# ConvFFN on one Trainium2 core: the last pair's block sums made by VectorE instead of by adding stores

## The chip, the cores and the metric

The kernel runs on one core of a Trainium2 chip. The metric is the device time of one execution in microseconds (us); less is better. TensorE (PE in the profile, its weight loads PEld) does the matmuls, VectorE (DVE) and ScalarE (ACT) the elementwise work, GpSimd (POOL) and SyncE (SP) mostly issue DMA transfers.

## The reference, cut to what matters

The program is a decoder trunk of two layers (attention mixes, then a ConvFFN in each). Only the ConvFFN is touched here, and it runs once in each layer:

```python
def conv_ffn(h, w_up, conv_w, conv_b, w_down):
    T = h.shape[1]
    a, b = jnp.split(h @ w_up, 2, axis=-1)
    a_pad = jnp.pad(a, ((0, 0), (CONV_WIDTH - 1, 0), (0, 0)))
    a = sum(a_pad[:, j:j + T] * conv_w[j] for j in range(CONV_WIDTH)) + conv_b
    return (jax.nn.silu(a) * b) @ w_down
```

Here T = 1024 tokens, the model width is 1024 and the inner width FFN_DIM is 2816, so 22 tiles of 128 channels.

## The kernel before

Both matrix products of the ConvFFN are done by a Strassen-like scheme with seven products in place of eight. The names `T1` to `T4` and `B11` to `B22` are the right-hand blocks and block sums of such a scheme; each product has its number (1 to 7).

**The up product.** A `Up` object ("unit") makes one tile of 128 inner channels of `a` and of `b` for both halves of the tokens (512 each). Its seven products are the methods `p1` to `p7`; each is 12 matmuls of 128x512 (four blocks of the contraction, and three matmuls a block, because every operand is split into a high and a low part). `sums` makes the sums of the weights that products 6, 7, 3 and 5 need, four DVE additions of 128x512 (L1042 to L1045). `split67` and `split35` split those sums into high and low parts. `p5` ends with a DVE instruction `summed` (L1103) that drains its PSUM tile `fw` into `s1`; product 3 adds on top of the same PSUM tile, so it may not start before that drain. `run` puts these calls of a unit and of the next one (`nxt`) in order.

**The gated blocks.** A unit ends with two gated blocks of 128x512, `c[0]` and `c[1]`, one for each half of the tokens (`gate`, DVE, L1160 and L1161). Units go in pairs, 11 pairs of a layer: the first of a pair has `mate` None, the second has the first as `mate`. Each pair leaves seven blocks in DRAM (`gb_d`): B11, T1, B21, B22, T2, T3, T4. Four of these are sums of up to four gated blocks. The kernel before makes the sums in DRAM: `store` writes a block (SP queue, L1167), and `more` adds another onto it (POOL queue, L1171, a DMA with `accum_op=ALU.add`). T4 gets all four blocks of its pair.

**The down product** is a loop over 77 steps, 7 products times 11 pairs, in the order of `DOWN` (L419): T4, B11, T2, B21, T3, T1, B22. A step is 12 matmuls (L1402 to L1404) into PSUM tiles `dn`. `load(i)` issues from SP, six steps ahead (`AHEAD`), the block `bl` from `gb_d` (L1266) and, in the first product, half of a weight tile `wb`, in the second a weight tile `wa` of 128x1024. `operand(i)`, three steps ahead (`READY`), makes the operands `da` (weights) and `db` (block): the high parts on ACT (L1326, L1331), the low parts on DVE (L1327, L1332). In the second product DVE also adds `wa` onto `wb` (L1294). Step 10 is the last step of the first product: it reads T4 of the last pair. Step 11 is the first that needs a `wa`. Four loads of `x` (L1352) go out between the load of step 10 and that of step 11.

**What sets the order.** The code names dependences and a scheduler places the instructions of each engine in one fixed list; an engine works its list strictly in order, so an instruction that waits holds up all behind it. SP's list too is one queue.

Of the kernel before, what the change touches and what calls it, by code (L numbers as in the profile page):

```python
# [11 lines left out]
ALU = mybir.AluOpType  # L12
# [22 lines left out]
def kernel(  # L35
# [25 lines left out]
    nc = tc.nc  # L61
# [19 lines left out]
    def PS(s="ps"):  # L81
        return pp.tile([P, HT], F32, tag="ps", name=nm(s))
# [7 lines left out]
    def hs(half):  # L90
        return slice(half * HT, (half + 1) * HT)
# [46 lines left out]
    def follow(n, after, reason):  # L138
        tc.add_manual_dep(
            n.ins,  # L140
            after.ins.name,
            mybir.DependencyInfo(mybir.DependencyClass.NoSync, mybir.DependencyReason.DATA),
            reason=reason,
        )
# [5 lines left out]
    def back_to_exp(after):  # L150
        follow(nc.scalar.preload_act_table_set(LN_EXP), after, "table")
# [827 lines left out]
    def ffn(l, blocks_, after):  # L979
# [25 lines left out]
        class Up:  # L1005
# [5 lines left out]
            def load(self, k=None):  # L1011
                if k is None:
                    self.load(0)
                    k = 1
                if k == 0:
                    self.raw = slot("raw", 2, raws)
                t = self.raw[k]
                for j in (1, 0) if self.early else (0, 1):
                    nc.sync.dma_start(t[:, hs(j)], w_up[l, j * NF + self.i, :, hs(k)])
# [85 lines left out]
            def p4(self):  # L1105
                ps = PS("fv")
                self.product(ps, 4, True, True)
                nc.vector.tensor_tensor(self.t, ps, self.t, ALU.add)
                self.ended = self.gate(0, self.t)
                if self.mate is None:  # L1110
                    self.stored = self.store(self.c[0], "B11", "T1", "T2", "T4")
                else:
                    self.stored = self.store(self.c[0], "B21")
                    self.more(self.c[0], "T4")

            def p3(self):
                self.product(self.W, 3, False, True)
# [28 lines left out]
            def end(self):  # L1146
                self.c.append(self.taps(self.q, self.edge))
                self.act(1)
                self.gate(1, self.s1)
                if self.mate is None:  # L1150
                    self.more(self.c[1], "T1", "T2", "T4")
                    self.store(self.c[1], "T3")
                else:
                    self.store(self.c[1], "B22")
                    self.more(self.c[1], "T2", "T3", "T4")

            def gate(self, half, t):
                c = self.c[half]
# [16 lines left out]
        def each(group, *whats):  # L1175
            for what in whats:
                for u in group:
                    getattr(u, what)()

        def ahead(then, after):  # L1180
            if after is not None:
                after.load(1)
            if then is not None and then.early:
                then.again()

        def run(u, last, then, after):
            nxt = [then] if then is not None else []
            if u.s1 is None:
                u.p1()
            u.p6()  # L1190
            if after is not None:
                after.load(0)
            if u.early:
                each(nxt, "direct")
                then.p1()
                each(last, "end")
                u.split35((then.kept, u.opened))
                ahead(then, after)
                u.p7()
                u.taps0()  # L1200
            else:
                u.p2()
                each(last[:1], "end")
                u.split35((u.kept, u.opened))
                ahead(then, after)
                u.p7()
                each(nxt, "direct")
            u.act0()
            each(nxt, "sums")
            u.p5()  # L1210
            for v in nxt:
                v.split67((u.acted, u.drained))
            if not u.early:
                each(last[1:], "end")
            u.p4()
            u.p3()
# [6 lines left out]
        seq = pair + order[:-1]  # L1223
        for n, u in enumerate(seq):
            u.n, u.mate = n // 2, seq[n - 1] if n % 2 else None
        each(pair, "load", "direct")
        each(pair, "p1")
        pair[0].p2()
# [18 lines left out]
        last = pair  # L1247
        for u, then, after_ in zip(order, order[1:], order[2:] + [None]):
            run(u, last, then, after_)
            last = [u]  # L1250
# [10 lines left out]
        tt = nc.vector.tensor_tensor  # L1261
# [146 lines left out]
        def down():  # L1408
            ps = {}
            for i in range(AHEAD):  # L1410
                load(i)
            for i in range(READY):
                operand(i)
            each(last, "end")
            back_to_exp(silu[0])
            yield 0.0
            for i, (p, n) in enumerate(steps):
                r = DOWN[p][0]
                if r == 3 and n == NP - TAIL:
                    break  # L1420
                if i + AHEAD < len(steps):
                    load(i + AHEAD)
                if n == 4 and p < 4:
                    fetch_x(*((0, range(4, 8)), (1, range(4)), (0, range(4)), (1, range(4, 8)))[p])
                which = "AB"[p % 2] if p < 5 else "B"
                if n == 0 and r not in (2, 3):
                    ps[which] = [PS("dn") for _ in range(4)]
                bank = ps[which]
                for m in range(4):
                    product(i, bank, (m,))  # L1430
                    if n == NP - 1:
                        if r == 5:
                            evac(r, m, bank[m])
                        else:
                            pend.append((r, m, bank[m]))
                if i + READY < len(steps):
                    operand(i + READY)
                if n != NP - 1 and pend:
                    evac(*pend.pop(0))
                yield 2.7  # L1440
            end_ = len(steps) - 1
            segs_ = [(t0 - HT, w) for t0, w in ends if t0 >= HT]
            bank = ps["B"]
            for t0, w in segs_:
                c = slice(t0, t0 + w)
                for m in range(4):
                    for i in range(end_ + 1 - TAIL, end_ + 1):
                        product(i, bank, (m,), c, i == end_)
                    xv = xs[m][:, HT + t0 : HT + t0 + w]
                    tt(xv, bank[m][:, c], xv, ALU.add)  # L1450
                    norm = nn[[e[0] for e in ends].index(HT + t0)]
                    if l == 0:
                        nc.scalar.dma_start(x_d[m, :, hs(1)], xv)
                    if l == 1 and m == 3:
                        norm.add_last(xv)
                    else:
                        norm.add(xv)
                    yield 0.65 * TAIL * w / HT
# [549 lines left out]
```

## Time and profile before

| what | us |
|---|---|
| median of 3 runs | 2266.38 (2264.17 to 2266.48) |
| profiled execution | 2264.45 |
| its span, first to last instruction | 2262.6 |
| PE busy | 2212.7 |
| DVE busy | 1713.2 |
| ACT busy | 1115.7 |
| POOL busy | 341.0 |

Times in the rows are microseconds from the start of the span. The first layer's down product begins at 844.80, the second's at 2029.89. In a row of the timeline the first number is the start, the second the duration; what stands in brackets is the engine's idle time before it and what ended it. A busy time of PE counts a matmul until its modelled end; matmuls overlap, and their starts, about 0.2265 us apart at full clock, are the better measure.

### The profile page before, as it was taken

To read this page: it belongs to the slowest core of one execution; us is meant where nothing else is said; L and a number is where in the kernel's file an instruction comes from. 1 tells how busy PE (TensorE), PEld (TensorE's weight loads), DVE (VectorE), ACT (ScalarE), POOL (GpSimd) and SP (SyncE) were. 2 spreads that over 40 slices of the span, in tenths; PEclk is the share of its full clock that TensorE was granted. 3 is DMA by queue.
4 is the path that set the end of the run, shared out by engine and by line. 5 is a ranking of instruction groups with operands and counts; after the bars stand their busy time and mean duration, and the time that the engine had idled before them with its cause. 6 is when DMAs were issued, how large, how long until landed. Compare 5 with 4: busy or idle time off the path is not lost.

```text
span 2262.6 us, 32372 instructions
## 1 busy us (share of the span) xinstructions
PE 2212.7 (98%) x11522; PEld 1844.6 (82%) x11522; DVE 1713.2 (76%) x3093; ACT 1115.7 (49%) x2085; POOL 341.0 (15%) x419
## 2 busy tenths in 40 slices
PE   9999999999999998999999999999999999999998
PEld 7888887777888887888888888888777888887886
DVE  6886876888777767877756778866988777767877
ACT  5564464543333334455544688874543333334445
POOL 1321300011111110000203223420012111110000
PEclk9999999999999999999999999999999999999999
DMA  6332246457866659543421111036457866659533
GB/s 226 103 103 87 64 164 206 139 168 191 195 159 154 147 137 325 182 135 131 145 83 49 50 46 38 8 115 209 141 168 192 195 161 145 162 137 325 163 97 112
DMA packets 161120, 325.60 MB, mean 144 GB/s; under 512 B 18173, under 2 KB 24910, under 8 KB 160958
## 3 DMA queue, kind: packets, MB, share of 16 engines
q1 hardware_dynamic: 130430, 263.11, 35.4%
q0 software_dynamic: 25776, 52.03, 13.4%
q10 hardware_dynamic: 4752, 8.39, 1.0%
q8 instruction: 90, 1.47, 0.3%
q14 instruction: 72, 0.59, 0.1%
HBM read 211.27 MB, written 112.20 MB: 143 GB/s over the span
## 4 chain that ended last, share of the span: by engine, by line
PE 76%; DVE 12%; DMA 5%; ACT 4%; issue 3%; SPq 0%; POOL 0%; DVEq 0%; ACTq 0%; POOLq 0%
PE dn L1403 5%; PE dn L1402 5%; PE dn L1404 5%; PE fx L1058 3%; PE fx L1060 3%; PE fx L1059 3%; PE fw L1058 3%; PE fw L1060 3%; PE fw L1059 3%; PE op L195 2%; PE op L196 2%; PE op L194 2%; DMA wu<-in_w_up_dram 2%; PE fy L1060 2%; PE fy L1059 2%
## 5 line engine op out<-in xcount | busy, mean ns | idle before, releaser
L1171 POOL DMA_DIRECT2D gb_d<-fc x154 | 134.0, 1130 | 913.1 <-DVE fc L1161 267.3
L1402 PE MATMUL dn<-db,da 128*128 128x512 f32 (+1 forms) x628 | 244.4, 389 | 10.2 <-ACT db L1331 10.2
L1403 PE MATMUL dn<-db,da 128*128 128x512 f32 (+1 forms) x628 | 243.6, 388 | 1.8 <-DVE db L1332 1.8
L1404 PE MATMUL dn<-db,da 128*128 128x512 f32 (+1 forms) x628 | 243.0, 387 | 0.0
L1022 ACT ACTIVATE Ah<-wu 128x1024 fp32r<-128x1024 f32 x124 | 130.2, 1052 | 120.1 <-PE fv L1059 55.0
L1023 DVE TENSOR_TENSOR Al<-wu,Ah 128x1024 fp32r<-128x1024 f32 x124 | 151.1, 1220 | 7.2 <-ACT Ah L1022 6.1
L1402 PEld LDWEIGHTS dn<-db,da 128*128 128x128 f32 x628 | 118.9, 189 | 36.0 <-ACT db L1331 11.9
L1058 PE MATMUL fw<-B,Ah 128*128 128x512 f32 x352 | 138.0, 392 | 4.7 <-DVE s L1103 4.7
L1403 PEld LDWEIGHTS dn<-db,da 128*128 128x128 f32 x628 | 118.8, 189 | 27.6 <-DVE db L1332 3.6
L1060 PE MATMUL fw<-B,Al 128*128 128x512 f32 x352 | 138.0, 392 | 0.0
L1404 PEld LDWEIGHTS dn<-db,da 128*128 128x128 f32 x628 | 118.7, 189 | 23.6
L1059 PE MATMUL fw<-B,Ah 128*128 128x512 f32 x352 | 137.1, 390 | 0.0
L1332 DVE TENSOR_TENSOR db<-bl,db 128x512 fp32r<-128x512 f32 x154 | 106.1, 689 | 36.7 <-ACT db L1331 36.1
L1331 ACT ACTIVATE db<-bl 128x512 fp32r<-128x512 f32 x154 | 95.4, 619 | 28.5 <-PE dn L1404 15.5
L194 PE MATMUL op<-om,wor 128*128 128x512 f32 x256 | 101.7, 398 | 0.8 <-ACT om L230 0.8
L195 PE MATMUL op<-om,wor 128*128 128x512 f32 x256 | 100.0, 391 | 0.9 <-DVE om L231 0.9
L196 PE MATMUL op<-om,wol 128*128 128x512 f32 x256 | 99.7, 390 | 0.0
L1144 ACT ACTIVATE fc<-fc 128x512 f32<-128x512 f32 x88 | 54.3, 626 | 74.1 <-DVE fc L1125 60.6
L1125 DVE SCALAR_TENSOR_TENSOR fc<-q,cs,fc 128x511 f32<-128x511 f32 x88 | 65.8, 748 | 24.4 <-ACT fc L1123 24.4
L1058 PEld LDWEIGHTS fw<-B,Ah 128*128 128x128 f32 x352 | 66.1, 188 | 21.0 <-DVE s L1103 7.7
L1058 PE MATMUL fx<-B,Ah 128*128 128x512 f32 x208 | 81.5, 396 | 1.4 <-ACT s L1082 1.4
L1022 ACT ACTIVATE A<-wu 128x512 fp32r<-128x512 f32 x44 | 27.7, 630 | 111.7 <-PE fx L1059 78.8
(428 smaller groups left out, 6366.9 us busy)
## 6 DMA issues: line engine op xcount, KB each, us to landing
wu<-in_w_up_dram SPq DMA_DIRECT2D x176, 256.0 KB, 3.7
gb_d<-fc SPq DMA_DIRECT2D x154, 256.0 KB, 6.1
gb_d<-fc POOLq DMA_DIRECT2D x154, 256.0 KB, 6.8
bl<-gb_d SPq DMA_DIRECT2D x154, 256.0 KB, 2.8
wb<-in_w_down_dram SPq DMA_DIRECT2D x44, 256.0 KB, 5.1
wa<-in_w_down_dram SPq DMA_DIRECT2D x22, 512.0 KB, 7.8
wo<-in_a_wo_dram SPq DMA_DIRECT2D x16, 512.0 KB, 3.7
xre<-om_d SPq DMA_DIRECT2D x32, 256.0 KB, 4.6
```

What stands on the lines that cost most here:

```text
L194: mm(ps, wr[:, k, :], hr, start=(k == 0), stop=False)
L195: mm(ps, wr[:, k, :], hl, start=False, stop=False)
L196: mm(ps, wl[:, k, :], hr, start=False, stop=(k == n - 1))
L1022: a = nc.scalar.activation(hi, src, AF.Copy)
L1023: b = nc.vector.tensor_tensor(lo, src, f(hi), ALU.subtract)
L1058: mm(ps, wr, hr, start=(first and j == 0), stop=False, skip_group_check=True)
L1059: mm(ps, wr, hl, start=False, stop=False, skip_group_check=True)
L1060: mm(ps, wl, hr, start=False, stop=(stop and j == 3), skip_group_check=True)
L1171: nc.gpsimd.dma_start(self.block(w), t, accum_op=ALU.add)
L1402: mm(o, hi, bh, start=first, stop=False, skip_group_check=True)
L1403: mm(o, hi, bl, start=False, stop=False, skip_group_check=True)
L1404: mm(o, lo, bh, start=False, stop=stop or n == NP - 1, skip_group_check=True)
```

## The change

For the pair that is last in its layer (`final`), only B11, T1 and B21 are stored early, and only one addition is left to an adding store (the second block of T1). The other sums are made on DVE by a new method `mixed`, called once in each layer, right behind the last unit's `end`: three additions of 128x512 in SBUF, T3 = B22 + `c[1]` of the first unit, T2 = T3 + B11, T4 = T2 + `c[0]` of the last unit. Four plain stores from SP follow: T4, T2, B22, T3. For this pair the SP stores stay seven and the adding stores go from seven to one, in each layer.

For the ten other pairs of a layer the blocks stay the same; T4 comes before T2 among the stores and additions, and the first unit's T3 is stored before its additions.

In `run` the call of `p5` moves ahead of the next unit's `sums`.

```diff
-                    self.stored = self.store(self.c[0], "B11", "T1", "T2", "T4")
+                    self.stored = self.store(self.c[0], "B11", "T1", *(() if self.final else ("T4", "T2")))
                 else:
                     self.stored = self.store(self.c[0], "B21")
-                    self.more(self.c[0], "T4")
+                    if not self.final:
+                        self.more(self.c[0], "T4")
...
                 if self.mate is None:
-                    self.more(self.c[1], "T1", "T2", "T4")
-                    self.store(self.c[1], "T3")
-                else:
+                    if not self.final:
+                        self.store(self.c[1], "T3")
+                    self.more(self.c[1], "T1", *(() if self.final else ("T4", "T2")))
+                elif not self.final:
                     self.store(self.c[1], "B22")
-                    self.more(self.c[1], "T2", "T3", "T4")
+                    self.more(self.c[1], "T4", "T2", "T3")
+
+            def mixed(self):
+                b11, b12 = self.mate.c
+                tt = nc.vector.tensor_tensor
+                tt(b12, self.c[1], b12, ALU.add)
+                tt(b11, b12, b11, ALU.add)
+                tt(self.c[0], self.c[0], b11, ALU.add)
+                self.store(self.c[0], "T4")
+                self.store(b11, "T2")
+                self.store(self.c[1], "B22")
+                self.store(b12, "T3")
...
             u.act0()
+            u.p5()
             each(nxt, "sums")
-            u.p5()
...
             each(last, "end")
+            each(last, "mixed")
```

How the instruction lists move. PE's list is the same in both kernels, row for row and tile for tile. So are the lists of DVE and ACT up to the end of the last pair, which means that the exchange of `p5` and `sums` in the code leaves the drain L1103 and the additions L1042 to L1045 where they were.

The first place is SP's list in the first layer, at the last pair's stores and the loads of steps 8 to 10. Before (`fc_963` is `c[1]` of the last unit, stored as B22; `wb_971`, `wb_972`, `wb_973` are the weights of steps 8, 9 and 10, `bl_950`, `bl_952`, `bl_954` the blocks of steps 8, 9 and 10):

```order
L1266 DMA wb_971_6788<-in_w_down_dram 128x512
L1167 DMA gb_d_97<-fc_963_6732 128x512
L1266 DMA bl_950_6700<-gb_d_97 128x512
L1266 DMA wb_972_6807<-in_w_down_dram 128x512
L1266 DMA bl_952_6704<-gb_d_97 128x512
L1266 DMA wb_973_6826<-in_w_down_dram 128x512
L1266 DMA bl_954_6708<-gb_d_97 128x512
```

Now (`fc_940` is T3, `fc_928` is T2, `fc_939` is T4):

```order
L1280 DMA wb_971_6785<-in_w_down_dram 128x512
L1180 DMA gb_d_97<-fc_963_6726 128x512
L1180 DMA gb_d_97<-fc_940_6614 128x512
L1280 DMA bl_950_6694<-gb_d_97 128x512
L1180 DMA gb_d_97<-fc_928_6478 128x512
L1180 DMA gb_d_97<-fc_939_6610 128x512
L1280 DMA wb_972_6804<-in_w_down_dram 128x512
L1280 DMA bl_952_6698<-gb_d_97 128x512
L1280 DMA wb_973_6823<-in_w_down_dram 128x512
L1280 DMA bl_954_6702<-gb_d_97 128x512
```

Three more stores stand behind that of B22, and the loads of steps 9 and 10 now come behind the store of T4.

The second place is DVE's list at the last unit's second gate. Before:

```order
L1160 TENSOR_TENSOR fc_963_6732<-fc_963_6732,s1_935_6581 128x512
L1327 SCALAR_TENSOR_TENSOR da_959_6720<-wb_955_6710,da_959_6720 128x512
L1332 TENSOR_TENSOR db_962_6727<-bl_956_6712,db_962_6727 128x512
L1327 SCALAR_TENSOR_TENSOR da_961_6726<-wb_964_6745,da_961_6726 128x512
L1332 TENSOR_TENSOR db_958_6715<-bl_946_6692,db_958_6715 128x512
```

Now:

```order
L1173 TENSOR_TENSOR fc_963_6726<-fc_963_6726,s1_935_6579 128x512
L1341 SCALAR_TENSOR_TENSOR da_959_6714<-wb_955_6704,da_959_6714 128x512
L1162 TENSOR_TENSOR fc_940_6614<-fc_963_6726,fc_940_6614 128x512
L1346 TENSOR_TENSOR db_962_6721<-bl_956_6706,db_962_6721 128x512
L1163 TENSOR_TENSOR fc_928_6478<-fc_940_6614,fc_928_6478 128x512
L1341 SCALAR_TENSOR_TENSOR da_961_6720<-wb_964_6742,da_961_6720 128x512
L1164 TENSOR_TENSOR fc_939_6610<-fc_939_6610,fc_928_6478 128x512
L1346 TENSOR_TENSOR db_958_6709<-bl_946_6686,db_958_6709 128x512
```

The three additions stand among the low parts of steps 5 and 6; the addition that makes T4 is the sixth instruction behind the gate.

The third place is ACT's list at the operands of steps 8 to 11. Before (`db_960` of `bl_954` is the high part of step 10's block, `da_969` of `wa_978` that of step 11's weights):

```order
L1326 ACTIVATE da_959_6720<-wb_972_6807 128x512
L1331 ACTIVATE db_962_6727<-bl_950_6700 128x512
L1326 ACTIVATE da_961_6726<-wb_973_6826 128x512
L1331 ACTIVATE db_958_6715<-bl_952_6704 128x512
L1331 ACTIVATE da_969_6764<-wa_978_6853 128x512
L1331 ACTIVATE db_960_6721<-bl_954_6708 128x512
```

Now:

```order
L1345 ACTIVATE db_962_6721<-bl_950_6694 128x512
L1340 ACTIVATE da_959_6714<-wb_972_6804 128x512
L1340 ACTIVATE da_961_6720<-wb_973_6823 128x512
L1345 ACTIVATE db_958_6709<-bl_952_6698 128x512
L1345 ACTIVATE db_960_6715<-bl_954_6702 128x512
L1345 ACTIVATE da_969_6761<-wa_978_6850 128x512
```

Step 10's block is now split ahead of step 11's weights; before it stood behind them.

More of the change, by code (lines that the diff above doesn't have):

```diff
@@ L1225, in ffn @@
             u.n, u.mate = n // 2, seq[n - 1] if n % 2 else None
+            u.final = n // 2 == len(seq) // 2 - 1
         each(pair, "load", "direct")
```

## The prediction

> **What bounds the kernel.** I read the page's busy times first, then the waits of PE, then PE's timeline at the places that the waits point to, and from there the queues that feed it.
>
> ```profile
> PE 2212.7 (98%) x11522; PEld 1844.6 (82%) x11522; DVE 1713.2 (76%) x3093; ACT 1115.7 (49%) x2085; POOL 341.0 (15%) x419
> ```
>
> PE is busy 98% of the span, and its work stays the same, so the change can only bring back what PE stands still or runs slowly: 2262.6 - 2212.7 = 49.9 us in all. The waits of PE (who waited for whom; us in total, times, longest) say which part of it lies near the change:
>
> ```profile
> PE dn L1402 <- ACT db L1331: 10.2, 4, 5.5
> PE fw L1058 <- DVE s L1103: 4.7, 7, 1.4
> PE dn L1403 <- DVE db L1332: 1.8, 4, 1.0
> ```
>
> The first and third are the down product waiting for the high and low parts of its blocks, the second is product 3 waiting for the drain of product 5. PE's timeline shows where the first sits. First layer, then second:
>
> ```profile
> 844.80 0.39 PE L1402 MATMUL dn<-db,da 128*128 128x512 f32 x1
> 850.01 0.39 PE L1404 MATMUL dn<-db,da 128*128 128x512 f32 x1
> ...
> 851.93 0.39 PE L1404 MATMUL dn<-db,da 128*128 128x512 f32 x1
> ...
> 873.06 0.39 PE L1404 MATMUL dn<-db,da 128*128 128x512 f32 x1
> 878.92 0.79 PE L1402 MATMUL dn<-db,da 128*128 128x512 f32 x1 [5.48 <-ACT db L1331]
> ...
> 883.68 0.39 PE L1404 MATMUL dn<-db,da 128*128 128x512 f32 x1
> ...
> 943.77 0.39 PE L1402 MATMUL dn<-db,da 128*128 128x512 f32 x1
> ...
> 947.82 0.39 PE L1402 MATMUL dn<-db,da 128*128 128x512 f32 x1
> ```
>
> ```profile
> 2029.89 0.39 PE L1402 MATMUL dn<-db,da 128*128 128x512 f32 x1
> ...
> 2035.11 0.39 PE L1404 MATMUL dn<-db,da 128*128 128x512 f32 x1
> ...
> 2037.35 0.40 PE L1404 MATMUL dn<-db,da 128*128 128x512 f32 x1
> ...
> 2058.45 0.39 PE L1404 MATMUL dn<-db,da 128*128 128x512 f32 x1
> 2062.28 0.50 PE L1402 MATMUL dn<-db,da 128*128 128x512 f32 x1 [3.44 <-ACT db L1331]
> ...
> 2067.74 0.39 PE L1404 MATMUL dn<-db,da 128*128 128x512 f32 x1
> ```
>
> From 844.80 to 850.01 are the 24 matmuls of steps 0 and 1, 23 intervals of 0.2265 us; a step is 2.72 us. Each pair of rows gives a loss, time between them less their intervals:
> - before step 2, three intervals (0.68): 851.93 - 850.01 - 0.68 = 1.24, and 2037.35 - 2035.11 - 0.68 = 1.56;
> - before step 10, twelve intervals to 883.68: 10.62 - 2.72 = 7.90; fifteen to 2067.74: 9.29 - 3.40 = 5.89;
> - at step 33, first layer alone: 947.82 - 943.77 - 2.72 = 1.33.
>
> The loss at step 10 is more than the idle time, since PE comes back slowly. In a table by stretches (PE, PEld, DVE, ACT, POOL busy, then the granted clock) the clock is at half:
>
> ```profile
> 880.00:882.00 2.00, 2.00 (x5) 1.54 (x6) 1.97 (x4) 1.22 (x3) 0.00 (x0) 0.50 1.03 398
> ```
>
> **Why step 10 is late.** The timeline of SP, POOL, ACT and DVE, first layer; the last two fences are DVE's and SP's of the second:
>
> ```profile
> 844.13 0.49 SPq L1266 DMA_DIRECT2D wb<-in_w_down_dram  x1
> ...
> 856.97 0.32 SPq L1167 DMA_DIRECT2D gb_d<-fc  x1
> ...
> 858.85 0.44 SPq L1266 DMA_DIRECT2D wb<-in_w_down_dram  x1
> 868.36 0.32 SPq L1266 DMA_DIRECT2D bl<-gb_d  x1
> ...
> 870.67 0.38 SPq L1266 DMA_DIRECT2D wa<-in_w_down_dram  x1
> ```
>
> ```profile
> 857.24 2.60 POOL L1171 DMA_DIRECT2D gb_d<-fc  x3 [7.45 <-DVE fc L1160]
> ```
>
> ```profile
> 849.52 0.63 ACT L1326 ACTIVATE da<-wb 128x512 fp32r<-128x512 f32 x1 [5.16 <-DMA wb<-in_w_down_dram]
> ...
> 868.61 0.63 ACT L1326 ACTIVATE da<-wb 128x512 fp32r<-128x512 f32 x1 [2.51 <-DMA wb<-in_w_down_dram]
> ...
> 877.72 0.63 ACT L1331 ACTIVATE da<-wa 128x512 fp32r<-128x512 f32 x1 [7.97 <-DMA wa<-in_w_down_dram]
> 878.26 0.61 ACT L1331 ACTIVATE db<-bl 128x512 fp32r<-128x512 f32 x1
> ```
>
> ```profile
> 856.26 0.69 DVE L1160 TENSOR_TENSOR fc<-fc,s 128x512 f32<-128x512 f32 x1
> ...
> 877.64 0.69 DVE L1294 TENSOR_TENSOR wb<-wa,wb 128x512 f32<-128x512 f32 x1 [6.56 <-DMA wa<-in_w_down_dram]
> ```
>
> ```profile
> 2041.43 0.69 DVE L1160 TENSOR_TENSOR fc<-fc,s 128x512 f32<-128x512 f32 x1
> ...
> 2061.00 0.69 DVE L1294 TENSOR_TENSOR wb<-wa,wb 128x512 f32<-128x512 f32 x1 [7.34 <-DMA wa<-in_w_down_dram]
> ```
>
> ```profile
> 2052.52 0.32 SPq L1266 DMA_DIRECT2D bl<-gb_d  x1
> ...
> 2054.83 0.38 SPq L1266 DMA_DIRECT2D wa<-in_w_down_dram  x1
> ```
>
> SP stands still from 859.3 to 868.36: its next entry is the load of T4, which waits for the last adding store. Everything behind it waits too, and `wa` goes out only at 870.67. ACT then holds step 10's block behind step 11's weights: `da<-wa` runs at 877.72, when `wa` has landed, and `db` at 878.26. So PE waits for `wa`, by way of two queues. Step 2 is a smaller thing of the same stage: its `wb`, issued at 844.13, reaches ACT at 849.52.
>
> **The change part by part.**
>
> *`p5` ahead of `sums`: 0.* The lists of PE and DVE are the same there, so the drain moves nowhere. It could be worth at most the 4.7 us of the second wait.
>
> *Six of seven adding stores go, in each layer.* POOL loses six DMA issues, which cost nothing (POOL waits for others all through this stage). What counts is when transfers land. The views of the two lines that store give the landing times over all transfers (min/median/max), plain stores from SP first, adding stores from POOL second:
>
> ```profile
> DMA to landing us min/median/max: 2.0/6.1/9.0
> ```
>
> ```profile
> DMA to landing us min/median/max: 3.9/6.8/10.9
> ```
>
> The same view, cut to single stores of the last pair, gives B22 at 856.97 first and then B21 of the second layer, which went out among adding stores:
>
> ```profile
> DMA to landing us min/median/max: 3.2/3.2/3.2
> ```
>
> ```profile
> DMA to landing us min/median/max: 5.6/5.6/5.6
> ```
>
> *Three additions on DVE.* They are of the form of the gate, 0.69 us each, one starting some 0.6 us behind the other. They stand in DVE's list at 857 to 861, where DVE idles later anyway until 877.64; 1.8 us in each layer, covered. Without that cover they would cost 1.8 each.
>
> *T4.* The addition that makes it is sixth behind the gate: 856.26 + 6 x 0.6 + 0.69 = 860.6, and SP's store goes out at 860.9. For its landing the bounds are 2.0 and 9.0; I take 3.2, the store nearest in place and size. Then the load of T4 goes out at 864.1, against 868.36. The step from it to `wa` keeps its 2.3 us: 866.4. `wa` took from 870.67 to 877.64, 7.0 us: it lands at 873.4. In the second layer the gate is at 2041.43, so the store at 2046.0 and T4 there at 2049.2; from the load of T4 to that of `wa` are 2.3 us, and `wa` took from 2054.83 to 2061.00, 6.2: it lands at 2057.7.
>
> *What step 11 can bear.* Without stalls it starts at 844.80 + 11 x 2.72 = 874.7. Its low part of the block is now the fourth DVE instruction behind the landing of `wa`, 2.5 us, and is wanted by the second matmul, at 874.95. So `wa` may land up to 872.4 here, and up to 2057.5 in the second layer. That leaves 1.0 and 0.2 us of stall. But the gate itself should come earlier: the taps ahead of it stand in DVE's list behind the operands of steps 2 and 3, which waited for `wb`. Two adding stores fewer stand ahead of that `wb`, and step 2's loss of 1.24 and 1.56 should go; half of it passed on to the gate (0.6 and 0.8) leaves 0.4 us in the first layer and nothing in the second.
>
> *Step 10 itself* is no longer behind `wa` on ACT: its block, loaded at 864.1 and some 3 us under way, is there before 872.0.
>
> *Step 33.* ACT stands still there for another thing, a weight of the next stage:
>
> ```profile
> 934.35 1.06 ACT L176 ACTIVATE wkcr<-wkc 128x1024 fp32r<-128x1024 f32 x1 [3.30 <-POOL wkc L169]
> ```
>
> In the new lists this instruction is three places (1.5 steps, 4.1 us) later on ACT, and its load one step (2.7 us) later on SP. Its wait shrinks by 1.4; I count half of the 1.33 us.
>
> *The new SP order* puts T3, T2 and T4 ahead of the loads of steps 9 and 10, which go out at about 861 and 862, 3 us later than now. They have until 867 (step 9 starts at 869.3); in the present trace the load at 858.85 reached ACT at 868.61, among the adding stores, and these are gone.
>
> *The ten other pairs of a layer* keep their counts of stores; T4 only goes out before T2. Their blocks are read in the down product, behind the last unit, and PE's waits show none of them but at step 10, so this costs nothing; without that distance it would show as waits of `dn` at earlier steps.
>
> *The sum:* 1.24 + 1.56 + 7.90 + 5.89 = 16.6, less 0.4, plus 0.7: 16.9 us. Against the profiled execution's 2264.45 that is 2247.6, against the median of 2266.38 it is 2249.5; the profiled one is at the fast end of the three. I say 2249.
>
> [...]
>
> **The rivals.**
>
> *The wait passes to `wa`.* T4 goes out in the thick of other stores and lands in L = 5.6 us, as B21 did in the second layer. With L us of landing `wa` is there at 860.9 + L + 2.3 + 7.0 = 870.2 + L in the first layer and at 2046.0 + L + 2.3 + 6.2 = 2054.5 + L in the second, so the stalls at step 11 are L - 2.2 and L - 3.0 before any help from an earlier gate: 3.4 and 2.6. For it speaks that four stores now go out within 4 us; against it that the adding stores are gone. The saving is 16.6 - 6.0 = 10.6: 2254 to 2256 by the two bases. Slow clock behind the stalls would cost 2.3 more in each layer (5.89 less the 3.60 by which the row at 2062.28 is late); then 6.0 is left: 2258 to 2260.
>
> The Trainium skill ("TensorE: Matmul & The Clock Gate", Part 1: The HAM clock gate) says that about 3.4 us of idle time bring the half clock. The trace agrees: 5.48 and 3.44 us of idle time were followed by it. By that rule stalls of 3.4 and 2.6 would bring it in one layer at most, and the time would be 2254 to 2258.
>
> *The stores hold up SP (the other side).* The same sum with a long L: stalls and slow clock take (L - 2.2) + (L - 3.0) + 4.6 = 2L - 0.6, against the 16.6 that go. From L = 8.6 the change gains nothing, and at 9.0, the slowest plain store, it is 0.8 slower. Slower by 0.2% needs L = 10.9, an adding store's worst: 2269 to 2271. For it speaks that a load behind SP's stand also took long (858.85, read by ACT at 868.61); against it the 3.2 of B22 in this very place.
>
> *The `p5` half does something after all.* Then up to 4.7 more go: 2244. Against it: the equal lists.
>
> **How the numbers follow.** A measurement of this kernel can tell about 0.2%, 4.5 us, from no change. Forecast (12 to 18 us saved): 0.70. Wait passed to `wa`, 4.5 to 12 saved: 0.17. Between 4.5 saved and 4.5 lost (L from 6.4 to 10.9): 0.08. Slower: 0.03. The `p5` half working: 0.02. Faster is 0.70 + 0.17 + 0.02 = 0.89, same 0.08, slower 0.03. The low end of the range is the profiled time less 16.6 and the whole 1.33, 2246.5, rounded down; the high end, 2258, takes in most of the passed wait. Together they leave out some 0.16.
>
> **What would show it.** In the trace after: no idle time of PE above 1 us near steps 2 and 10 of either layer and the clock at 1.00 throughout the stage; SP's load of T4 some 4 us earlier behind the first step; `wa` landing less than 27.6 us behind the first matmul of the down product; PE's waits for `s` (L1103) still near 4.7 us. The prediction is wrong if PE's wait moves to step 9 or 11, or if T4's store lands in over 6 us.

## The result, and the profile after

The kernel after takes 2252.05 us (median of four runs, 2248.05 to 2255.76), the kernel before 2265.86 beside it: a ratio of 0.994, 95% interval 0.992 to 0.996. That is 13.8 us less; 2249 was forecast, with a range of 2246 to 2258. The profiled execution took 2255.76 us (span 2253.7) and was the slowest of the four.

The page's busy times, and PE's waits (who waited for whom; us in total, times, longest):

```profile
PE 2211.4 (98%) x11522; PEld 1844.8 (82%) x11522; DVE 1715.6 (76%) x3099; ACT 1116.9 (50%) x2085; POOL 330.5 (15%) x407
```

```profile
PE fw L1058 <- DVE s L1103: 6.9, 7, 2.0
```

The down product (`dn`), first on that list before with 10.2 us for its high parts, is no longer among the top ones; the drain of product 5 now leads. PE's timeline, at the first matmul of the down product and at the starts of steps 2 and 11, the first layer and then the second:

```profile
847.24 0.39 PE L1416 MATMUL dn<-db,da 128*128 128x512 f32 x1
...
852.67 0.39 PE L1416 MATMUL dn<-db,da 128*128 128x512 f32 x1
...
877.15 0.39 PE L1416 MATMUL dn<-db,da 128*128 128x512 f32 x1
...
1060.41 0.39 PE L1418 MATMUL dn<-db,da 128*128 128x512 f32 x1
```

```profile
2028.41 0.39 PE L1416 MATMUL dn<-db,da 128*128 128x512 f32 x1
...
2033.85 0.39 PE L1416 MATMUL dn<-db,da 128*128 128x512 f32 x1
...
2058.33 0.39 PE L1416 MATMUL dn<-db,da 128*128 128x512 f32 x1
...
2240.65 0.28 PE L1418 MATMUL dn<-db,da 128*128 128x256 f32 x1
```

From step 0 to step 11 are 132 intervals, 29.90 us at full clock; the rows are 29.91 and 29.92 apart. Steps 2 and 10 lose nothing in either layer. From the first row of each fence to the last is the length of the down product: 213.17 and 212.24 us. Before, by the same two matmuls, it was 221.55 and 219.76. So 8.4 + 7.5 = 15.9 us came out of the two stages.

Of these, the profiled execution gave some back elsewhere: the up products took 430.0 and 429.2 us against 427.3 and 426.0 before, the stretch between the layers 538.8 against 537.5. The sum, -15.9 + 2.7 + 3.2 + 1.3 - 0.2, is the -8.9 of the spans. The loss in the up product stands at two places; the first of them, with the clock of both behind it (busy times of PE, PEld, DVE, ACT, POOL, then granted clock, DMA share, GB/s):

```profile
530.50 0.39 PE L1060 MATMUL fv<-B,Al 128*128 128x512 f32 x1
532.81 0.55 PE L1058 MATMUL fw<-B,Ah 128*128 128x512 f32 x1 [1.93 <-DVE s L1103]
```

```profile
533.00:536.00 3.00, 3.00 (x8) 2.37 (x8) 3.00 (x5) 0.00 (x0) 2.05 (x3) 0.52 1.23 175
1714.00:1717.00 3.00, 3.00 (x8) 2.31 (x8) 3.00 (x5) 0.00 (x0) 2.02 (x3) 0.52 1.07 175
```

Product 3 waits 1.93 us for the drain, and half a clock for 3 us follows. The lists at that place are those of before, so the change of the lists does not explain it; the experiments return to it.

SP and ACT in the first layer, the rows that answer to those of the prediction:

```profile
860.64 1.52 SPq L1180 DMA_DIRECT2D gb_d<-fc  x2
...
864.65 0.32 SPq L1280 DMA_DIRECT2D bl<-gb_d  x1
...
866.97 0.38 SPq L1280 DMA_DIRECT2D wa<-in_w_down_dram  x1
```

```profile
869.41 0.63 ACT L1345 ACTIVATE db<-bl 128x512 fp32r<-128x512 f32 x1 [1.32 <-DMA bl<-gb_d]
874.73 0.63 ACT L1345 ACTIVATE da<-wa 128x512 fp32r<-128x512 f32 x1 [4.69 <-DMA wa<-in_w_down_dram]
```

T2 and T4 are stored from 860.64; the load of T4 goes out at 864.65, 17.4 us behind the first step (before 23.6); `wa` is there for ACT at 874.73, 27.5 us behind it, 0.1 us inside the limit of 27.6 that the prediction set.

The DMA queues are a part of the profile that the prediction did not read for this stretch. From 4 us ahead of the first step to the start of step 10 as it would be without stalls, 31.2 us; packets, MB, share of the 16 DMA engines' time; before, then after:

```profile
q1 hardware_dynamic: 3421, 6.24, 59.5%
q0 software_dynamic: 1008, 1.84, 34.6%
```

```profile
q1 hardware_dynamic: 4355, 8.45, 78.8%
q0 software_dynamic: 144, 0.26, 7.1%
```

The software queue is POOL's. Before, its seven adding stores took 34.6% of 31.2 us, 10.8 us of all 16 engines, 1.54 each; the other transfers got 6.24 MB through. After, one adding store is left, and the others get 8.45 MB through in the same time. The share adds up the times of the packets that start in the stretch; packets can overlap, so the sum of the queues can pass 100%.

### The profile page after: what moved, and what is told of

It is laid out like the page before. It is cut to its first block, busy times and chain, and to the rows that moved or that the text cites. A ratio compares the mean times of both kernels' runs of the same rounds, so it can differ in the third digit from the quotient of the medians.

```text
span 2253.7 us, 32334 instructions
## 1 busy us (share of the span) xinstructions
PE 2211.4 (98%) x11522; PEld 1844.8 (82%) x11522; DVE 1715.6 (76%) x3099; ACT 1116.9 (50%) x2085; POOL 330.5 (15%) x407
## 4 chain that ended last, share of the span: by engine, by line
PE 80%; DVE 10%; DMA 3%; ACT 3%; issue 2%; SPq 0%; POOL 0%; DVEq 0%; ACTq 0%; POOLq 0%
PE dn L1417 5%; PE dn L1418 5%; PE dn L1416 5%; PE fx L1058 3%; PE fx L1060 3%; PE fx L1059 3%; PE fw L1058 3%; PE fw L1060 3%; PE fw L1059 3%; PE op L195 3%; PE op L196 2%; PE op L194 2%; PE fy L1060 2%; PE fy L1059 2%; PE fy L1058 2%
## 5 line engine op out<-in xcount | busy, mean ns | idle before, releaser
L1184 POOL DMA_DIRECT2D gb_d<-fc x142 | 123.5, 1125 | 891.1 <-DVE wu L1043 299.8
```

Of the source, the lines that this page charges most:

```text
L1184: nc.gpsimd.dma_start(self.block(w), t, accum_op=ALU.add)
```

## The experiments

The theory of the prediction (A): SP's wait for T4 and the order on ACT make the stall. The rival that the experiments raised (D): the adding stores take the DMA engines' time, so that all loads land late, waited for or not. The expectations of the first four runs also name theories B and C. The length of the down product, measured as above, is the cleanest result; medians and ratios stand beside it. The "fw" column is the total of PE's waits for the drain.

| kernel | down product, us | up product, us | fw, us | median, us | ratio to before, 95% |
|---|---|---|---|---|---|
| before | 221.6, 219.8 | 427.3, 426.0 | 4.7 | 2262 to 2266 | |
| after | 213.2, 212.2 | 430.0, 429.2 | 6.9 | 2252.05 | 0.994 (0.992 to 0.996) |
| after, again | 213.0, 212.3 | 427.9, 426.2 | 5.5 | 2246.69 | 0.9923 (0.9907 to 0.9939) |
| last pair alone changed | 212.4, 212.2 | 427.0, 426.7 | 5.1 | 2246.54 | 0.9916 (0.9901 to 0.993) |
| sum tied behind the drain | 212.2, 212.2 | 425.6, 423.7 | 0.5 | 2244.16 | 0.9905 (0.9888 to 0.9922) |
| the same again | 212.2, 212.6 | 425.8, 423.3 | 0.3 | 2242.19 | 0.9916 (0.9903 to 0.9929) |
| before, T4 first | 217.9, 216.9 | 428.6, 429.6 | 7.8 | 2258.82 | 0.9972 (0.996 to 0.9984) |
| before, step 10 on B11 | 217.7, 216.2 | 427.8, 426.5 | 5.4 | 2256.28 | 0.9971 (0.9959 to 0.9982) |
| before, `wa` ahead of T4 | 220.3, 219.5 | 428.2, 426.1 | 4.1 | 2264.3 | 1.0002 (0.9992 to 1.0012) |
| before, ACT's order changed | 220.6, 220.4 | 431.1, 428.8 | 7.2 | 2264.0 | 1.0004 (0.9993 to 1.0014) |
| after, six adding stores back | 218.8, 217.2 | 429.9, 426.2 | 5.2 | 2260.41 | 0.9986 (0.9976 to 0.9997) |
| after, six plain stores more | 214.8, 214.0 | 428.3, 425.3 | 3.7 | 2248.6 | 0.994 (0.9923 to 0.9956) |
| before, four adding stores less | 214.7, 214.3 | 428.1, 427.0 | 6.4 | 2250.98 | 0.9948 (0.9933 to 0.9964) |

The length of a stage hides where in it the time goes. The next table gives PE's loss by place, first and second layer: the time between the first matmuls of two steps, less 2.72 us a step. There is one profile of each kernel.

| kernel | steps 2 to 4, us | steps 8 to 13, us | steps 31 to 36 (first layer alone), us |
|---|---|---|---|
| before | 1.3, 1.6 | 7.9, 5.9 | 1.3 |
| after | 0, 0 | 0.1, 0 | 2.0 |
| before, T4 first | 1.6, 2.1 | 2.5, 2.5 | 2.8 |
| before, step 10 on B11 | 3.7, 2.4 | 0.4, 1.4 | 2.5 |
| before, `wa` ahead of T4 | 2.2, 1.8 | 6.0, 5.5 | 1.2 |
| before, ACT's order changed | 1.6, 1.4 | 6.8, 6.8 | 1.2 |
| after, six adding stores back | 2.2, 4.3 | 3.2, 0.8 | 2.3 |
| after, six plain stores more | 0.8, 0.5 | 0.6, 1.3 | 2.2 |
| before, four adding stores less | 0.5, 0.4 | 1.0, 1.4 | 2.0 |

**The kernel after, again.**

> The changed kernel once more, for a second profile and the spread of its time. In its first profile the stage around the start of the down product gave back 15.7 us, but the span fell by 8.9 only: in the up product PE's seven waits for s (L1103) had grown from 4.7 to 6.9 us, and behind two of them, 1.9 and 2.0 us long, the clock stood at half. Theory A (the extra loss is chance: where a weight load lands a little late, the drain comes late, and a wait of 2 us may or may not bring the slow clock): the waits differ again, the time lies between 2248 and 2256, and PE loses nothing at steps 2 and 10. Theory B (T4 ahead of T2 among the adding stores of the other ten pairs makes weight loads late each time): the same two long waits and 2254 or more.

The stages of the down product repeat to 0.2 us; the up products are 2.1 and 3.0 us shorter than in the first profile, at the level of before. With the lists of before in this part (all rows but the two with the tied sum), the first layer's up product lies anywhere from 427.0 to 431.1 and the second's from 425.3 to 429.6. The 430.0 and 429.2 of the first profile lie within that spread, so its loss is taken for chance, and 2246.69 shows the change better than 2252.05 does.

**The last pair alone.** From after: the other ten pairs keep the old order of their stores, and `p5` stands behind the sums.

```diff
-self.store(self.c[0], "B11", "T1", *(() if self.final else ("T4", "T2")))
+self.store(self.c[0], "B11", "T1", *(() if self.final else ("T2", "T4")))
...
-    self.more(self.c[1], "T4", "T2", "T3")
+    self.more(self.c[1], "T2", "T3", "T4")
...
-u.p5()
 each(nxt, "sums")
+u.p5()
```

> The sums on VectorE for the last pair alone; the other ten pairs keep the old order of stores and additions, and p5 stands behind sums as before. The instruction lists are those of the changed kernel, but for which block of DRAM a store of the other pairs goes to. Theory A: the time of the changed kernel run beside it, to within 2 us. Theory B: 4 to 6 us less than the changed kernel, and PE's seven waits for s (L1103) near 4.7 us with none over 1.5.

As after, to 0.8 us in each stage of the down product: all of the gain sits in the last pair's seven blocks.

**The third sum tied behind the drain.** From after; this makes true what the exchange of `p5` and `sums` says.

```diff
-def sums(self):
+def sums(self, past=None):
...
-    tt(a0, b1, a0, ALU.subtract)
+    third = tt(a0, b1, a0, ALU.subtract)
+    if past is not None:
+        follow(third, past, "order")
...
-each(nxt, "sums")
+for v in nxt:
+    v.sums(u.summed)
```

> The changed kernel, with the second half of its code made true in the lists: the third of the four sums of weights is tied behind the drain of product 5 (L1103), so that at most two of the four stand ahead of it. Two sums of 0.6 us then leave the way of the drain. Theory A: PE's seven waits for s shrink by up to 1.3 us each, none is long enough for the slow clock, 4 to 8 us less than the changed kernel (2244 to 2248), and less spread. Rival C (the sums are now late for the next unit's splits, and with them products 6 and 7): waits of fy or fz on Ah or Al take their place, and the time is that of the changed kernel or longer.

And its second run:

> The kernel after with the third weight sum of each unit tied behind the drain of product 5, unchanged from its first run, to see whether its lead over the kernel after holds. If the tie is worth something: up stages again near 425.6 and 423.7 us (the kernel after had 430.0 and 429.2, then 427.9 and 426.2), no or one wait of product 3 for the drain, ratio 0.989 to 0.992. If the first lead was chance: up stages of 427 or more and a ratio of 0.992 to 0.994.

PE's waits for the drain in the first of these runs and in the second:

```profile
PE fw L1060 <- DVE s L1105: 0.5, 1, 0.5
```

```profile
PE fw L1060 <- DVE s L1105: 0.3, 1, 0.3
PE fw L1061 <- DVE B L231: 0.2, 1, 0.2
```

Both runs have the two shortest up products of all kernels in both layers, 1.2 to 2.0 us below the shortest of the others. So the idea behind the `p5` half is worth some 1 to 3 us a layer, but only if the scheduler is told. The ratios of these kernels and of after overlap; the lengths of the up product do not. Beside the kernel after, run again, the first of the two is 2.5 us faster; the expectation said 4 to 8. The tie also moves rows in other lists (64 places of PE's list differ), so the gain is that of the whole new order. This is the fastest version run.

**Before, with T4 first.** The stores and adding stores of all pairs in the order T4, T2, as after; all sums still by adding stores. The lists stay but for the block that a store writes.

> The kernel before, with nothing but the order of stores and additions of the change: T4 first, in all eleven pairs, by adding stores; no sum on VectorE. The lists of instructions are those of the kernel before. If the wait for T4 at SP is the cause and its length follows from the third adding store of the last unit landing in 10.0 us (the first landed in 7.1), the load of T4 goes out some 3 us earlier in the first layer and 1 to 2 in the second, and PE's stall at step 10 shrinks as much: 3 to 6 us less than before, 2259 to 2263. The loss at step 2 stays at 1.2 and 1.6. Rival D (the adding stores as a load on the DMA engines, and not the order of one wait, make wa late): no change to 1 us.

It gains 3.6 and 2.9 us in the stages, where theory D alone had expected no change to 1 us. T4's last adding store is first and no longer third on POOL: by the view of the single stores it landed 5.6 us after its issue, against 10.0 before. SP's load of T4, with the first step at 842.96, is

```profile
861.53 0.32 SPq L1266 DMA_DIRECT2D bl<-gb_d  x1
```

18.6 us behind the first step, not 23.6 (19.3 and not 22.6 in the second layer). The loss at step 2 stays. Order alone is less than half of the change by the stages, but it takes away 5.4 and 3.4 us of the loss at steps 8 to 13; some of that is lost again elsewhere.

**Before, with nobody waiting for T4.** Step 10 reads B11 of the last pair, stored long before.

```diff
-fetch(i, raw_ring[i % AHEAD], gb_d[n, BLK.index(blk)])
+fetch(i, raw_ring[i % AHEAD], gb_d[n, BLK.index("B11" if i == NP - 1 else blk)])
```

> The kernel before, with one change of data: step 10 reads block B11 of the last pair, which is stored long before, in place of T4. All adding stores stay and all instruction lists stay as they were; the product of step 10 is computed on the wrong block. Theory A (SP's wait for T4, passed on to the load of step 11's weights and from there to ACT, is the whole stall): SP goes on at about 860, the weights land at 867 to 869, the losses at step 10 (7.9 and 5.9 us) go, step 2 keeps its 1.2 to 1.6 us; down stages near 213.7 and 213.9 us in place of 221.6 and 219.8; time about 13.8 us less (ratio 0.994). Rival D (the adding stores load the DMA rings, so that the weights come late even where nobody waits for T4): weights later than 873, both down stages over 216, less than half of the gain.

Theory A as it was put, that the wait is the whole stall, fails here: the wait is gone, and the stages give back 3.9 and 3.6 us, not 7.9 and 5.9. But at steps 8 to 13 the loss does fall, from 7.9 and 5.9 to 0.4 and 1.4. What the stages do not give back lies at steps 31 to 36 (1.1 us more than before) and at step 2, which lost 2.4 and 0.8 us more, though it comes some 8 us before the first load that the edit changes.

A PE that is late from step 2 also needs its loads later, so the gain at step 10 is partly owed to that. With the loss at step 2 of before it would have stood some 1.7 us at step 10 (an estimate from this trace: ACT is done with the block at 873.84, and PE would have come to it at 872.2). Counted from the first step up to step 14, PE lost 9.2 and 7.5 us before and 4.1 and 3.8 here: about half of the loss goes with the wait. The loads are late all the same. SP (two rows) and ACT, first layer, first step at 843.7:

```profile
858.08 0.45 SPq L1266 DMA_DIRECT2D wb<-in_w_down_dram  x1
...
864.12 0.33 SPq L1266 DMA_DIRECT2D wa<-in_w_down_dram  x1
```

```profile
864.16 0.63 ACT L1326 ACTIVATE da<-wb 128x512 fp32r<-128x512 f32 x1 [2.04 <-DMA wb<-in_w_down_dram]
...
868.21 0.63 ACT L1326 ACTIVATE da<-wb 128x512 fp32r<-128x512 f32 x1 [2.90 <-DMA wb<-in_w_down_dram]
...
872.68 0.63 ACT L1331 ACTIVATE da<-wa 128x512 fp32r<-128x512 f32 x1 [3.31 <-DMA wa<-in_w_down_dram]
```

The `wb` issued at 858.08 lands at 868.2, after 10 us, though no one holds it up (in the kernel after, the same load is issued at 863.21 and ACT has it at 866.94); and SP stands again, 2.3 us until 864.12, now for the `wb` ahead of it, which lands at the moment ACT's row at 864.16 shows:

```profile
SPq L1266 <- DMA wb<-in_w_down_dram: 2.3, 1, 2.3
```

The queues over the same 31.2 us:

```profile
q1 hardware_dynamic: 3953, 7.46, 67.7%
q0 software_dynamic: 1008, 1.84, 33.9%
```

Together they take 101.6% of the DMA engines' time, against 94.1% before and 85.9% after; by this measure the engines are full. With the one wait gone, SP runs up against the next load that has not landed.

**Before, with `wa` ahead of T4's load; and with ACT's order changed.** In the first, `load` issues the weights of step 11 just before step 10's block. In the second, two ties put ACT's split of `wa` behind `db` of step 10, and DVE's sum L1294 behind its low part.

```diff
-elif r == 1:
+elif r == 1 and n:
...
+if i == NP - 1:
+    wa[0] = V(s="wa")
+    fetch(i, wa[0], w_down[l, seq[0].i])
 if i < AHEAD:
```

```diff
+if i == NP and k == 4:
+    follow(a, tenth[0], "order")
+elif i == NP - 1 and k == 3:
+    tenth[:] = a, b
...
+if i == NP:
+    follow(b, tenth[1], "order")
```

> The kernel before with one load moved: SP issues the weights of step 11 just ahead of the load of step 10's block, and no longer behind it. The adding stores, T4 and its wait stay. Theory A: the weights land near 867, step 10 waits at most for its own block (T4's load out at 868.4, landed 871.4, split by 872.7, wanted from 873.2 with step 2's loss of 1.2 in between): 0 to 0.8 us of loss in a layer; down stages 213.7 to 214.5 and 213.9 to 214.5; 12 to 13.8 us less, ratio 0.994 to 0.995, from one moved load. Rival E (T4 itself is too late, whatever stands behind it): a loss of 3 us or more stays at step 10 in each layer and the gain is under 8 us.

> The kernel before with one order changed: ACT splits step 10's block ahead of step 11's weights, and DVE's weight sum of step 11 stands behind the low part of that block. SP's list keeps T4's load ahead of the weights' load, so these still land at 877.6 and 2061.0. Theory A: step 10 runs on time, and the wait moves to step 11, where it is smaller, since 2.7 us of work stand between: about 2.3 to 3.9 us in the first layer and 0.5 to 1.9 in the second, and no half clock in the second; 8 to 11 us less (ratio 0.995 to 0.9965). Rival F (the order on ACT is of no account, the weights' landing alone sets the time): the loss at step 11 is as large as that at step 10 was, less than 3 us gained.

Neither changes the time; theory A had expected 12 to 13.8 us less of the first and 8 to 11 of the second. SP in the first kernel, the weights of step 11 and, behind T4's load, those of step 12:

```profile
855.81 0.81 SPq L1266 DMA_DIRECT2D wa<-in_w_down_dram  x1
865.11 0.33 SPq L1266 DMA_DIRECT2D bl<-gb_d  x1
...
867.90 0.38 SPq L1266 DMA_DIRECT2D wa<-in_w_down_dram  x1
```

PE in the first layer at the start of step 11, first kernel, then second, and the clock behind the latter:

```profile
875.90 0.50 PE L1405 MATMUL dn<-db,da 128*128 128x512 f32 x1 [2.88 <-ACT db L1334]
```

```profile
877.72 0.76 PE L1409 MATMUL dn<-db,da 128*128 128x512 f32 x1 [2.87 <-ACT db L1332]
```

```profile
880.00:882.00 2.00, 2.00 (x6) 1.60 (x5) 2.00 (x5) 1.15 (x2) 0.00 (x0) 0.50 1.03 399
```

With `wa` ahead, step 10 is on time (`wa` lands at 865.2), but T4's load holds the next `wa`, that of step 12, which goes out at 867.90 and lands at 874.6. ACT's list has the split of those weights (874.70) ahead of step 11's block (875.23), as it had step 11's weights ahead of step 10's block: the stall moves to step 11, 4.2 and 3.8 us of it, and a stretch at half clock follows. With ACT's order changed, step 10 is on time too and the stall also stands at step 11, 4.4 us and then half clock. Both chains that the prediction named are there, and cutting one link moves the stall by one step, since the weights behind T4's load land no sooner.

**After, with the six adding stores put back where nobody waits; and with six plain ones.** From after, a method `ghost` stores the last pair's tiles from POOL onto blocks of the two pairs before; the plain version leaves out `accum_op`.

```diff
+def ghost(self, t, back, *whats):
+    for w in whats:
+        nc.gpsimd.dma_start(gb_d[self.n - back, BLK.index(w)], t, accum_op=ALU.add)
...
+    self.ghost(self.c[0], 1, "B21")
...
+    self.ghost(self.c[1], 1, "T1", "B22")
...
+    self.ghost(self.c[1], 2, "T1", "B22", "B21")
```

> The kernel after, and with it the six adding stores per layer that it had dropped: same tiles, same size, same places in the code, but onto blocks of the two pairs before (T1, B22, B21), which are read much later. Nobody waits for them, T4 is still made by VectorE, and the lists of PE, DVE, ACT and SP stay as after. The last pairs' products are computed on altered blocks. Theory D (the adding stores' share of the DMA engines is what the stage lacks: the six take some 9 us of all 16 engines, and the kernel after leaves some 2.5 to 4 us free in the 27 us up to step 10): down stages 217 to 219 and 216 to 218 us against 213.2 and 212.2 after, stalls at steps 2 and 10 or 11 again, 8 to 11 us slower than after, ratio 0.995 to 0.998. Theory A (the waits for T4 at SP and the order on ACT): down stages near 213 and 212.5, ratio 0.992.

> As the run with the six extra adding stores, but the six simply write and do not add: the same bytes from POOL, a store of 256 KB at 0.75 us of 16 engines (by the hardware queue's rows) in place of 1.54. The last pairs' products are computed on altered blocks. Theory D with the price in the adding: 4.5 us of DMA time more in a stage with 2.5 to 4 us free: 0 to 2 us lost in each layer, down stages 213 to 215, ratio 0.992 to 0.994. Theory D with the price in POOL's queue, whatever it does: as with the adding stores, 216 to 219. Theory A: no loss, 213 and 212.5.

The software queue in the same 31.2 us, adding stores, then plain ones (both with the one adding store onto T1 that is left):

```profile
q0 software_dynamic: 1008, 1.84, 42.4%
```

```profile
q0 software_dynamic: 624, 1.84, 20.5%
```

PE's waits in the down product, adding stores (two rows), then plain ones:

```profile
PE dn L1426 <- ACT db L1355: 4.6, 4, 2.0
PE dn L1427 <- DVE db L1356: 3.1, 7, 0.8
```

```profile
PE dn L1427 <- DVE db L1356: 2.4, 5, 0.8
```

The lists of PE, DVE, ACT and SP are those of after, T4 is made by DVE, and no one reads the six blocks soon. Yet the stages are 5.6 and 5.0 us longer: steps 2, 9 and 11 stall in the first layer, steps 2 and 11 in the second. T4's plain store now takes its time too: by the view of that one store it lands 8.4 us after its issue, against 2.7 in the kernel after, and SP's load of T4 goes out 24.6 us behind the first step (869.08 against 844.5), later than before the change. So this run brings the wait back by way of the load on the DMA engines; it shows what the adding stores cost, and does not part the two theories. With the same bytes as plain stores 1.6 and 1.8 us are lost, a third. An adding store takes 1.5 to 1.9 us of all 16 DMA engines (13.2 us over seven here, 10.8 over seven before), a plain one some 0.8 (20.5% of 31.2 is 6.4 us, less the one adding store, over six). The Trainium skill ("DMA: Bandwidth & Descriptors", Rules for kernel authors) says that an accumulating transfer reads its destination and writes it later; it gives no price. By these rows it takes about twice the DMA time of a plain store.

**Before, without four of the seven adding stores**, those onto T1, T2, T2 and T3; the three onto T4 stay.

```diff
-self.more(self.c[1], "T1", "T2", "T4")
+self.more(self.c[1], *(("T4",) if self.final else ("T1", "T2", "T4")))
...
-self.more(self.c[1], "T2", "T3", "T4")
+self.more(self.c[1], *(("T4",) if self.final else ("T2", "T3", "T4")))
```

> The kernel before, without four of the seven adding stores of the last pair: those onto T1, T2, T2 and T3 are left out, the three onto T4 stay, and so do SP's wait for T4 and all lists but POOL's. T1, T2 and T3 of the last pair hold sums that lack a block. Theory D: some 6 us of DMA time less, three of the four within the stage: down stages 216 to 218 and 215.5 to 217.5 (before 221.6 and 219.8), weights behind T4's load in 6 us or less in place of 7; ratio 0.996 to 0.9975. Theory A: the wait stays, and only the last adding store onto T4 goes out 1.7 us earlier, as it is first and no longer third on POOL: 1.5 to 2 us less in each layer, ratio 0.998 to 0.9985.

It beats its expectation under both theories: 214.7 and 214.3 us, 6.8 and 5.5 less than before, with T4 made by adding stores as ever. Two things differ from before: four adding stores are gone, and the last one onto T4 is now first on POOL, as in the run with T4 first. The queue, and SP's loads of T4 and `wa` (first step at 840.2):

```profile
q0 software_dynamic: 432, 0.79, 14.5%
```

```profile
858.29 0.32 SPq L1267 DMA_DIRECT2D bl<-gb_d  x1
...
860.61 0.38 SPq L1267 DMA_DIRECT2D wa<-in_w_down_dram  x1
```

T4's load goes out 18.1 us behind the first step, 5.5 sooner than before. The run with T4 first, with all adding stores, already had it at 18.6, so nearly all of that is the place on POOL (in the second layer 17.7, against 19.3 there and 22.6 before). What the four missing stores are worth shows against that run: the stages are 3.2 and 2.6 us shorter, and the loss at step 2 falls from 1.6 and 2.1 to 0.5 and 0.4. From here to the kernel after 1.5 and 2.0 us are left; T4 made by VectorE, the adding stores still here and the new order of the lists share them, and no run parts these.

## Why the prediction was right, and where its reasons were not

**The size of the gain held.** The losses at steps 2 and 10, 16.6 us by PE's rows, went whole, in the five profiles of kernels with `mixed` and no stores added. The sum of 16.9 stands against 15.9 in the stages and 13.8 to 16.9 in the medians (after, after again, last pair alone, each against the runs of before beside it).

**The path held, in the main.** SP held up by T4 and ACT by `wa` are both there. With the wait for T4 alone gone, about half of what PE lost up to step 14 went (5.1 of 9.2 us, 3.7 of 7.5). With either of the two other links cut, the stall moved by one step and the time stayed. Step 2 was put down to adding stores ahead of its `wb`, and that held: its loss stays in every kernel that keeps the adding stores of before (1.3 to 3.7 us), and falls to 0.5 and 0.4 with four of them gone.

**One term was missing.** The step that failed is "POOL loses six DMA issues, which cost nothing ... What counts is when transfers land". The issues cost nothing, but the transfers do: six adding stores take some 9 us of all 16 engines in each layer (6 x 1.54), in a stretch where the queues together took 94%, and 102% as soon as nobody waited. Put back alone they cost 5.6 and 5.0 of the 8.4 and 7.5 us; four of them left out, with T4 first, give 3.2 and 2.6. The prediction names the effect on the `wb` of step 2, on the loads of steps 9 and 10 and, among the rivals, on T4's landing, but its sum has no term for it; T4's plain store landed in 2.7 us with those stores gone and took 8.4 with them back. The sum came out because it was made of what PE lost, whatever the cause, and because this change removes the wait and the load at once. That part is luck.

**T4's route.** Its store was to land in 3.2 us, its load to go out 19.3 us behind the first step, `wa` to land by 27.6. The store landed in 2.7, the others came at 17.4 and 27.5. Two sizes were off and partly cancelled: the load of T4 was 1.9 us early, while `wa` took 7.8 us from its issue, not 7.0, with nearly all adding stores gone. So not every load gets faster without them. The residue of 0.4 did not come. The rival with the long landing names what happened when the adding stores were put back: T4's plain store landed late and the stall came.

**Step 33.** The +0.7 did not come; the loss grew. Over steps 31 to 36 of the first layer PE lost 2.0 us in the profile of after (0.85 and 0.55 in one piece at steps 32 and 34), 1.3 before, and 1.1 to 1.9 in the other four profiles without added stores. These 0.7 us are the difference between the 16.6 that went and the 15.9 in the stages; why the loss grew is not shown.

**`p5` ahead of `sums`: 0** held for the change as written, and so did the equal lists.

**What the sum did not hold** is the up product, 5.9 us longer in the first profile and 0.7 in the second. The range covered it. PE's wait for the drain, which was to stay near 4.7 us, was 6.9 in the first profile and 5.5 and 5.1 in the next two.

## What to carry to other kernels

When a stage stalls on late loads, read the DMA share and each queue's part of it for that stretch beside who waits for whom; where the engines are full, cutting one wait gave back half here, and cutting a link behind it only moved the stall. Look at where in a stage each run loses its time before judging a cause by the length of the stage. An adding store cost about two plain ones of DMA time, so let an engine with idle time make the sums where transfers are dense; where that cannot be done, put the sum that is read first at the head of the adding stores. An order written in code is worth something only where the instruction lists show it, or where it is tied.

## What the hardware showed that was not expected

- The half clock came after far shorter idle times than the 3.44 us seen before: after 1.93 and 1.95 us in the up product of after, after 2.87 us in the run with ACT's order changed, and after 1.29 + 0.22 us at step 2 of the run on B11 (first layer). It did not come after 1.45 + 0.23 us at the same place of the run with six adding stores back, nor after a wait of 1.87 us in the second up product of that run. The Trainium skill ("TensorE: Matmul & The Clock Gate", What's actually happening) puts it at about 3.4 us of idle window; these runs do not bear that out as a threshold for one gap.
- A load that nobody holds up took 10 us among adding stores (issued 858.08, used 868.21), and SP's queue stood 2.3 us at another that had not landed.
- Three adding stores issued within 1.1 us of each other landed one after the other, some 2 us apart: in the last unit before, 7.1, 8.5 and 10.0 us after issues 0.54 us apart.
